# Twelve softmax scalings go from VectorE to GpSimd in a fused two-layer transformer kernel

## The chip, the cores and the metric

The kernel runs on one core of one Trainium2 chip. The metric is the device time of one execution in microseconds, as the median of three runs. Engine names are those of the profile: PE is TensorE (PEld its weight loads), DVE is VectorE, ACT is ScalarE, POOL is GpSimd, and SP is the engine that issues most DMAs.

## The reference

Two transformer layers work on 512 tokens of width 1024. The first layer mixes tokens by a spatial gating unit, the second by causal attention with a forgetting gate; both also have four heads of attention over 256 memory vectors, and both end in a gated feed-forward part. The change touches the second layer's attention alone, which has 12 heads of width 64:

```python
def forgetting_attention(q, k, v, log_f):
    c = jnp.cumsum(log_f, axis=1)
    ...
    def block(args):                       # one of four blocks of 128 query tokens
        logits = jnp.einsum('bthd,bshd->bhts', qi, k).astype(jnp.float32) * scale
        logits = logits + ci[..., :, None] - cT[..., None, :]
        logits = jnp.where(mask, logits, -jnp.inf)
        p = jax.nn.softmax(logits, axis=-1).astype(v.dtype)
        return jnp.einsum('bhts,bshd->bthd', p, v)
```

Everything is float32.

## The kernel before

**Products.** A float32 product is made of three matmuls on parts: each operand is split into a high part, cast by ACT (`whi`, L275), and a low part, the rest, subtracted by DVE (`wlo`, L276). Such a triple is what L218 to L220 show. The splits of weights, queries, keys and transposed softmax rows are most of the work of ACT and DVE.

**A forgetting head** (`FoxHead`) works on four token blocks `tb` = 0 to 3 of 128 queries each. Since attention is causal, block `tb` has rows of 128·(`tb`+1) keys, so block 3 is the longest, 128x512. The steps of a head are these.

- S3, S2, S1, S0 (`logits`): two matmuls make the block's logits `lg` in PSUM (L534, L535); one DVE instruction adds the mask, writes the rows to a tile `p` in SBUF and takes their maximum `nmx` (L543); ACT makes the exponential in place and its sum `sm` (L545). Block 0 lies in the same tile as block 2.
- N2 and N0 (`norm`; N3 and N1 do nothing): DVE takes the reciprocal of two blocks' sums at once (L477) and scales each block's rows by it (L479), the higher block first. N2 serves blocks 3 and 2, N0 serves 1 and 0.
- T0, T1, T2 (`transpose`, `turn`): PE turns the 128x128 pieces of `p` into a PSUM tile `tr` (L486), from which ACT and DVE make the parts `pT`. T0 takes the first key block of all four token blocks, so it needs all of N2 and N0; T1 and T2 take the rest.
- V0, V1, V2 (`values`): PE multiplies `pT` with the values into `o` (L559). ACT and DVE bring `o` to the tile `f` (L454, L455).

**Order.** `attend` writes the steps of head n and of head n−1's T and V steps into one list, with pieces of other matmul work (projections of queries, keys and values in the early heads, `qk` and `v`; the output projection, `y`, in the late ones) put between them. The framework's scheduler then sets each engine's order from dependencies and its own costs; each engine runs its own queue in that order and waits at semaphores.

```python
steps = ("T0", "S3", "F0", "T1", "S2", "N3", "F1", "V0", "S1", "N2", "T2", "F2", "S0", "N1", "V1", "N0",
         "F3", "V2", "F4")
```

**GpSimd** has little in this stage: for each head two small DMAs (`head_sums`, L1570 and L1571) that bring the gate's sums to the tiles `qc` and `kc` for the head after next, each held until the older head's logits have been read.

Functions that the diff touches, with the profile's line numbers (in the changed kernel, lines behind the two new ones are one or two higher: L479 becomes L480, L486 L487, L534 L536, L543 L545, L545 L547, L559 L561):

Of the kernel before, what the change touches and what calls it, by code (L numbers as in the profile page):

```python
# [43 lines left out]
def hybrid(ctx: ExitStack, tc: tile.TileContext, i: dict, out: bass.AP):  # L44
# [36 lines left out]
    V, A, PE, G = nc.vector, nc.scalar, nc.tensor, nc.gpsimd  # L81
# [209 lines left out]
    class Norm:  # L291


        def __init__(self, width=T):
            self.r4 = small("r4")
            self.acc, self.width = None, width
# [161 lines left out]

    class Softmax:


        def __init__(self):
            self.nmx, self.sm = small("nmx"), small("sm")
# [9 lines left out]
        def norm(self, tb):  # L473

            if tb % 2:
                return
            V.reciprocal(self.sm[:, tb : tb + 2], self.sm[:, tb : tb + 2])  # L477
            for x in (tb + 1, tb):
                V.tensor_scalar_mul(self.p[x], self.p[x], self.sm[:, x : x + 1])  # L479

        def turn(self, n, pieces):

# [9 lines left out]
    class MemHead(Softmax):  # L492
# [15 lines left out]
        def transpose(self, b):  # L508
            self.turn(b, [self.p[tb][:, b * P : (b + 1) * P] for tb in range(TB)])
# [10 lines left out]
    class FoxHead(Softmax):  # L520

        TURNS = ((0,), (1, 3), (2,))

        def __init__(self, pr, j, vals, dst):
            super().__init__()
# [22 lines left out]
        def transpose(self, b):  # L548
            self.turn(b, [self.p[tb][:, sb * P : (sb + 1) * P] for sb in self.TURNS[b] for tb in range(sb, TB)])

        def values(self, b):
            if b == 0:
                self.o = ps("mm", s="o")
            at = 0
            for sb in self.TURNS[b]:
                n = T - sb * P
# [1188 lines left out]
```

## Time and profile before

| | |
|---|---|
| time, median of 3 runs | 1086.39 us (1085.83 to 1086.45) |
| time of the profiled execution | 1085.8 us |
| its span, first to last instruction | 1084.1 us, at a granted clock of 0.998 |
| PE, DVE, ACT, POOL busy, share of the span | 99%, 87%, 68%, 7% |
| the 12 forgetting heads | about 598 to 706 us of the span |
| DVE busy in these 108 us | 97.94 us |
| POOL busy in these 108 us | 13.05 us |

A row of the timeline gives the start in us, the duration in us, the engine, the line, the operation, output and inputs, the shape, and how many like instructions were merged; idle time of the engine ahead of it and what ended that stand in brackets. A matmul's end is modelled, so the pace of PE is read from starts. On DVE too an instruction's duration overlaps the start of the next a little, so its cost to the queue is the distance from start to start.

### The profile page before, as it was taken

To read this page: it belongs to the slowest core of one execution; us is meant where nothing else is said; L and a number is where in the kernel's file an instruction comes from. 1 tells how busy PE (TensorE), PEld (TensorE's weight loads), DVE (VectorE), ACT (ScalarE), POOL (GpSimd) and SP (SyncE) were. 2 spreads that over 40 slices of the span, in tenths; PEclk is the share of its full clock that TensorE was granted. 3 is DMA by queue.
4 is the path that set the end of the run, shared out by engine and by line. 5 is a ranking of instruction groups with operands and counts; after the bars stand their busy time and mean duration, and the time that the engine had idled before them with its cause. 6 is when DMAs were issued, how large, how long until landed. Compare 5 with 4: busy or idle time off the path is not lost.

```text
span 1084.1 us, 19973 instructions
## 1 busy us (share of the span) xinstructions
PE 1074.6 (99%) x7224; PEld 981.8 (91%) x7224; DVE 944.6 (87%) x1893; ACT 737.1 (68%) x1605; POOL 72.7 (7%) x98
## 2 busy tenths in 40 slices
PE   9999999999999999999999999999999999999997
PEld 7998889999999988998988998889999999988996
DVE  7889659999989999986987899959999988999975
ACT  8776468766666677666765677758766666667563
POOL 0101011000000000000110111001000000000000
PEclk9999999999999999999999999999999999999999
DMA  7456666967664976364441754535867653646332
GB/s 274 160 143 167 192 166 199 247 180 209 165 179 144 272 207 215 107 202 130 128 128 47 208 128 114 151 98 185 242 196 195 165 160 115 174 130 202 107 118 78
DMA packets 131835, 179.52 MB, mean 166 GB/s; under 512 B 9948, under 2 KB 93928, under 8 KB 131736
## 3 DMA queue, kind: packets, MB, share of 16 engines
q1 hardware_dynamic: 119608, 160.66, 47.0%
q0 software_dynamic: 11712, 17.40, 10.1%
q8 instruction: 57, 0.93, 0.4%
q14 instruction: 42, 0.34, 0.1%
q10 hardware_dynamic: 416, 0.18, 0.1%
HBM read 158.71 MB, written 43.00 MB: 186 GB/s over the span
## 4 chain that ended last, share of the span: by engine, by line
PE 93%; issue 2%; DVE 2%; ACT 1%; DMA 1%; POOL 0%; SPq 0%; POOLq 0%; DVEq 0%; ACTq 0%
PE a L218 7%; PE a L219 7%; PE a L220 7%; PE y L218 4%; PE y L219 4%; PE y L220 4%; PE e L218 4%; PE e L219 3%; PE e L220 3%; PE ps L218 3%; PE ps L220 3%; PE ps L219 3%; PE p L218 3%; PE p L220 3%; PE p L219 3%; PE x L218 3%
## 5 line engine op out<-in xcount | busy, mean ns | idle before, releaser
L276 DVE TENSOR_TENSOR wlo<-raw,whi 128x512 fp32r<-128x512 f32 x316 | 211.0, 686 | 21.6 <-ACT whi L275 18.2
L275 ACT CAST whi<-raw 128x512 fp32r<-128x512 f32 x316 | 189.0, 618 | 57.8 <-PE a L219 15.0
L218 PE MATMUL a<-xshi,whi 128*128 128x256 f32 x480 | 135.2, 282 | 0.0
L219 PE MATMUL a<-xslo,whi 128*128 128x256 f32 x480 | 134.9, 281 | 0.0
L220 PE MATMUL a<-xshi,wlo 128*128 128x256 f32 x480 | 134.7, 281 | 0.0
L275 ACT CAST whi<-room 128x512 fp32r<-128x512 f32 x160 | 98.2, 621 | 48.1 <-PE x L219 9.6
L276 DVE TENSOR_TENSOR wlo<-room,whi 128x512 fp32r<-128x512 f32 x160 | 108.8, 687 | 6.4 <-ACT whi L275 3.9
L218 PEld LDWEIGHTS a<-xshi,whi 128*128 128x128 f32 x480 | 90.3, 188 | 1.8 <-ACT e L1119 1.0
L219 PEld LDWEIGHTS a<-xslo,whi 128*128 128x128 f32 x480 | 90.4, 188 | 0.7
L220 PEld LDWEIGHTS a<-xshi,wlo 128*128 128x128 f32 x480 | 90.4, 188 | 0.0
L218 PE MATMUL ps<-xshi,whi 128*128 128x256 f32 x192 | 54.3, 288 | 0.3 <-ACT whi L275 0.2
L220 PE MATMUL ps<-xshi,wlo 128*128 128x256 f32 x192 | 53.9, 284 | 0.0
L219 PE MATMUL ps<-xslo,whi 128*128 128x256 f32 x192 | 53.8, 282 | 0.0
L275 ACT CAST ff<-u 128x256 fp32r<-128x256 f32 x80 | 32.3, 406 | 29.1 <-PE p L220 15.1
L218 PE MATMUL y<-whi,mixedhi 128*128 128x512 f32 x128 | 51.2, 400 | 0.0
L219 PE MATMUL y<-wlo,mixedhi 128*128 128x512 f32 x128 | 50.7, 396 | 0.0
L218 PE MATMUL p<-whi,ff 128*128 128x512 f32 x128 | 50.5, 396 | 0.0
L220 PE MATMUL y<-whi,mixedlo 128*128 128x512 f32 x128 | 50.4, 394 | 0.0
L219 PE MATMUL p<-wlo,ff 128*128 128x512 f32 x128 | 50.3, 393 | 0.0
L220 PE MATMUL p<-whi,ff 128*128 128x512 f32 x128 | 50.2, 395 | 0.0
L219 PE MATMUL x<-xslo,whi 128*128 128x256 f32 x160 | 45.1, 282 | 0.0
L219 PE MATMUL e<-t,whi 128*128 128x256 f32 x160 | 45.1, 282 | 0.0
(376 smaller groups left out, 3573.5 us busy)
## 6 DMA issues: line engine op xcount, KB each, us to landing
room<-in_w_up SPq DMA_DIRECT2D x36, 512.0 KB, 4.1
raw<-in_w_gate SPq DMA_DIRECT2D x24, 512.0 KB, 4.3
raw<-in_w_down SPq DMA_DIRECT2D x20, 512.0 KB, 4.4
sums<-in_w_gate SPq DMA_DIRECT2D x16, 512.0 KB, 6.0
sums<-in_w_gate POOLq DMA_DIRECT2D x16, 512.0 KB, 7.0
raw<-in_w_out SPq DMA_DIRECT2D x16, 512.0 KB, 3.9
sums<-in_w_down SPq DMA_DIRECT2D x32, 256.0 KB, 5.4
sums<-in_w_down POOLq DMA_DIRECT2D x16, 512.0 KB, 7.8
```

The lines of the kernel that those rows point to most:

```text
L218: PE.matmul(o, w[0], x[0], start=start, stop=False, skip_group_check=more)
L219: PE.matmul(o, w[0], x[1], start=False, stop=False, skip_group_check=more)
L220: return PE.matmul(o, w[1], x[0], start=False, stop=stop, skip_group_check=more)
L275: last_hi[0] = A.copy(hi, src)
L276: last_split[0] = last_hi[0], (eng or V).tensor_sub(lo, src, hi)
```

## The change

The scaling of block 3 of each forgetting head, a 128x512 instruction, is issued on GpSimd; blocks 2, 1 and 0 stay on VectorE, and so do the memory heads.

```diff
     class Softmax:
 
+        by_pool = None
 
         def __init__(self):
...
             V.reciprocal(self.sm[:, tb : tb + 2], self.sm[:, tb : tb + 2])
             for x in (tb + 1, tb):
-                V.tensor_scalar_mul(self.p[x], self.p[x], self.sm[:, x : x + 1])
+                (G if x == self.by_pool else V).tensor_scalar_mul(self.p[x], self.p[x], self.sm[:, x : x + 1])
...
     class FoxHead(Softmax):
 
         TURNS = ((0,), (1, 3), (2,))
+        by_pool = 3
```

What it does to the queues is read from the order of the built programs. On GpSimd, from the DMAs for head 1 on, there stood DMAs alone:

```order
L1570 DMA qc_7663<-cc 2x512
L1571 DMA kc_7665<-cc 2x512
L1570 DMA qc_7662<-cc 2x512
L1571 DMA kc_7664<-cc 2x512
L1570 DMA qc_7663<-cc 2x512
L1571 DMA kc_7665<-cc 2x512
```

The same place now, heads 0 and 1 (`p_7820` and `p_7931` are their blocks 3, `sm_7671` and `sm_7673` the reciprocals):

```order
L1572 DMA qc_7663<-cc 2x512
L1573 DMA kc_7665<-cc 2x512
L480 TENSOR_SCALAR p_7820<-p_7820,sm_7671 128x512
L1572 DMA qc_7662<-cc 2x512
L1573 DMA kc_7664<-cc 2x512
L480 TENSOR_SCALAR p_7931<-p_7931,sm_7673 128x512
L1572 DMA qc_7663<-cc 2x512
L1573 DMA kc_7665<-cc 2x512
```

One scaling a head has come between the pairs of DMAs, twelve in all, and DVE has twelve instructions fewer. Up to head 6 the order of PE and ACT is as before and DVE differs by little more than those instructions; from head 7 on the scheduler set the engines' orders anew. On VectorE, before, from head 9's N2 (`p_8907`, `p_8930`) to its N0 (`p_8957`, `p_8930`); `p_9020` is head 10's block 3:

```order
L479 TENSOR_SCALAR p_8907<-p_8907,sm_7689 128x512
L479 TENSOR_SCALAR p_8930<-p_8930,sm_7689 128x384
L543 ISA p_8930,nmx_7688<-lg_8974,mask 128x128
L543 ISA nmx_7688 128x1
L455 TENSOR_TENSOR f_8997<-o_8951,f_8997 64x512
L276 TENSOR_TENSOR wlo_9077<-raw_9074,whi_9076 128x512
L477 RECIPROCAL sm_7689<-sm_7689 128x2
L543 ISA p_9020,nmx_7690<-lg_9017,mask 128x512
L543 ISA nmx_7690 128x1
L479 TENSOR_SCALAR p_8957<-p_8957,sm_7689 128x256
L479 TENSOR_SCALAR p_8930<-p_8930,sm_7689 128x128
```

And the same place now:

```order
L480 TENSOR_SCALAR p_8930<-p_8930,sm_7689 128x384
L545 ISA p_8930,nmx_7688<-lg_8974,mask 128x128
L545 ISA nmx_7688 128x1
L276 TENSOR_TENSOR wlo_9077<-raw_9074,whi_9076 128x512
L455 TENSOR_TENSOR f_8997<-o_8951,f_8997 64x512
L478 RECIPROCAL sm_7689<-sm_7689 128x2
L276 TENSOR_TENSOR wlo_9081<-raw_9074,whi_9080 128x512
L480 TENSOR_SCALAR p_8957<-p_8957,sm_7689 128x256
L480 TENSOR_SCALAR p_8930<-p_8930,sm_7689 128x128
L545 ISA p_9020,nmx_7690<-lg_9017,mask 128x512
```

The 512-wide scaling is gone, head 10's masking now comes behind N0 and not ahead of it, and a weight split (`wlo_9081`) has come ahead. On PE, before, ahead of head 9's T0 (`tr_9008`); `lg_9058` is head 10's S1:

```order
L220 MATMUL y_9048<-whi_8870,mixedlo_7316 128x512
L218 MATMUL y_9048<-whi_8874,mixedhi_7543 128x512
L219 MATMUL y_9048<-wlo_8875,mixedhi_7543 128x512
L220 MATMUL y_9048<-whi_8874,mixedlo_7544 128x512
L534 MATMUL lg_9058<-ka_8934,qa_8933 128x256
L535 MATMUL lg_9058<-kc_7664,qc_7662 128x256
L218 MATMUL y_9048<-whi_8880,mixedhi_8040 128x512
L486 MATMUL tr_9008<-ident,p_8930 128x128
L486 MATMUL tr_9008<-ident,p_8957 128x128
```

And now:

```order
L220 MATMUL y_9048<-whi_8870,mixedlo_7316 128x512
L487 MATMUL tr_9008<-ident,p_8930 128x128
L487 MATMUL tr_9008<-ident,p_8957 128x128
L487 MATMUL tr_9008<-ident,p_8930 128x128
L487 MATMUL tr_9008<-ident,p_8907 128x128
L487 MATMUL tr_9033<-ident,p_8957 128x128
L487 MATMUL tr_9033<-ident,p_8930 128x128
L487 MATMUL tr_9033<-ident,p_8907 128x128 x2
L218 MATMUL y_9048<-whi_8874,mixedhi_7543 128x512
```

Four 512-wide and two 256-wide matmuls that stood ahead of the turn now stand behind it. In the same way the next head's two logits matmuls have gone behind T0 in heads 7 (256 wide), 8 and 10 (512 wide), in head 7 with one 512-wide matmul of a key projection.

## The prediction

> **What bounds the kernel now.** I read the page's totals and its chain first, then the busy time by stretches of the forgetting heads, then who waited there. The page, parts 1 and 4:
>
> ```profile
> PE 1074.6 (99%) x7224; PEld 981.8 (91%) x7224; DVE 944.6 (87%) x1893; ACT 737.1 (68%) x1605; POOL 72.7 (7%) x98
> PE 93%; issue 2%; DVE 2%; ACT 1%; DMA 1%; POOL 0%; SPq 0%; POOLq 0%; DVEq 0%; ACTq 0%
> ```
>
> PE sets the time: 93% of the chain that ended last. A modelled busy share proves little by itself, so I look at the stage. Busy time by stretch (start and end; length; then PE, PEld, DVE, ACT, POOL):
>
> ```profile
> 611.00:635.00 24.00, 24.00 (x145) 21.23 (x144) 23.42 (x68) 18.21 (x46) 3.47 (x6) 1.00 0.64 169
> 662.50:695.00 32.50, 32.41 (x178) 27.05 (x177) 32.01 (x91) 27.85 (x70) 3.17 (x6) 1.00 0.58 154
> sum 108.00, PE 107.91 PEld 95.91 DVE 97.94 ACT 79.70 POOL 13.05; mean PE 21.58 PEld 19.18 DVE 19.59 ACT 15.94 POOL 2.61
> ```
>
> In heads 1 to 3 (611 to 635 us) and 7 to 10 (662.5 to 695) DVE is full as well, with 0.58 and 0.49 us free. So DVE could be the engine that holds PE. The waits of PE's weight loads between 598 and 706 us, which stand for PE's own, tell whether it does (total, times, longest):
>
> ```profile
> PEld tr L486 <- PE lg L535: 0.5, 1, 0.5
> PEld o L559 <- DVE pT L276: 0.4, 2, 0.3
> PEld o L559 <- ACT pT L275: 0.4, 1, 0.4
> ```
>
> They come to 1.3 us in four waits. DVE is full but just keeps up. That is the most a freer DVE can give back here, 0.12% of the time: the upper bound of any gain.
>
> **What goes from DVE.** The twelve scalings as one group (busy, mean ns of one), and one of them with the instruction behind it:
>
> ```profile
> L479 DVE TENSOR_SCALAR p<-p,sm 128x512 f32<-128x512 f32 x12 | 5.8, 481 | 0.1
> 687.85 0.48 DVE L479 TENSOR_SCALAR p<-p,sm 128x512 f32<-128x512 f32 x1
> 688.25 0.68 DVE L276 TENSOR_TENSOR pT<-tr,pT 128x512 fp32r<-128x512 f32 x1
> ```
>
> From start to start one costs the queue 0.40 us, so 12 x 0.40 = 4.8 us leave DVE. Beside PE's work this is worth nothing by itself; it counts only where PE waits for DVE.
>
> **What comes to GpSimd.** The trace has no scaling on GpSimd. The nearest rows are its passes over SBUF tiles, and rows where it met DVE:
>
> ```profile
> 2.08 0.61 POOL L105 TENSOR_SCALAR_AFFINE_SELECT tri<-ones 128x512 fp32r<-128x512 f32 x1
> 38.26 1.10 POOL L726 TENSOR_SCALAR_AFFINE_SELECT wsf<-wsf 128x768 f32<-128x768 f32 x1 [2.09 <-DMA wsf<-in_w_sp]
> ...
> 37.22 0.69 DVE L395 TENSOR_TENSOR q<-q,q 64x512 fp32r<-64x512 f32 x1
> ...
> 38.66 1.24 DVE L395 TENSOR_TENSOR q<-q,q 64x512 fp32r<-64x512 f32 x1
> ...
> 718.51 0.69 DVE L276 TENSOR_TENSOR wlo<-raw,whi 128x512 fp32r<-128x512 f32 x1
> 718.68 0.96 POOL L289 TENSOR_TENSOR r<-v,mhalf 128x1 f32<-128x1 f32 x1 [37.17 <-DVE v L889]
> ```
>
> One scaling takes GpSimd between 0.61 us (a like pass over the same size) and 1.10 us (a pass over a tile half as wide again, with a wait in it). I take 0.61, the nearest in size. The Trainium skill ("GPSIMD Engine Reference", section 4.1) says that one-input work runs there at roughly line rate; with its 1.2 GHz I estimate 0.43 us for 512 elements, and then DVE would stand less and the sum below would end nearer its lower end. No row here goes that low.
>
> The rows also show that the two engines block each other. DVE's subtraction at 38.66, with two inputs in SBUF, took 1.24 us and not 0.69 while GpSimd went over its tile, and ended 0.54 us after it: it stood until GpSimd was done. The other way round, GpSimd's small power at 718.68 took 0.96 us behind a split that ended at 719.20. So the 0.40 us saved is set against DVE standing behind GpSimd. Per head this lies between 0 (GpSimd runs beside a mask or a `pT`, whose first input is in PSUM) and 1.10 (a split or a scaling behind all of it). By the order, a 384-wide scaling or a split stands next to it in nearly every head. I take 0.20 to 0.40: a third to two thirds of 0.61. DVE's net gain per head is then 0 to 0.2 us, and PE is left as it is.
>
> **Is block 3 ready in time?** The rows around the end of heads 7 and 8, the reciprocal of N2, the scalings of N0 and PE's T0:
>
> ```profile
> 667.33 0.16 DVE L477 RECIPROCAL sm<-sm 128x2 f32<-128x2 f32 x1
> ...
> 669.38 0.53 DVE L479 TENSOR_SCALAR p<-p,sm 128x256 f32<-128x256 f32 x2
> ...
> 670.36 1.03 PE L486 MATMUL tr<-ident,p 128*128 128x128 f32 x8
> ...
> 675.42 0.54 DVE L479 TENSOR_SCALAR p<-p,sm 128x256 f32<-128x256 f32 x2
> ...
> 676.27 1.04 PE L486 MATMUL tr<-ident,p 128*128 128x128 f32 x8
> ```
>
> The two logits matmuls and the one `qk` matmul that now stand behind head 7's T0 are worth 2 x 0.12 + 0.23 = 0.47 us (paces in the rows of the next fence), so PE asks for block 3 at 669.89, 2.4 us after the reciprocal's end at 667.49. GpSimd needs at most a split's 0.69 us of waiting and 1.10 of work, 1.8. It is in time, and its two DMAs for later heads, queued behind the scaling, are late by no more than that, for logits a whole head later.
>
> **The turn moved ahead.** T0 also needs N0, whose chain is mask, exponential, reciprocal, scaling. Heads 9 and 10, with PE's pace in the logits matmuls:
>
> ```profile
> 684.52 0.40 ACT L545 ACTIVATE p<-p,nmx 128x128 f32<-128x128 f32 x1
> 685.05 0.17 DVE L477 RECIPROCAL sm<-sm 128x2 f32<-128x2 f32 x1
> 685.15 0.69 DVE L543 CUSTOM_DVE_ANT_0 p<-lg,mask 128x512 f32<-128x512 f32 x1
> 685.77 0.55 DVE L479 TENSOR_SCALAR p<-p,sm 128x256 f32<-128x256 f32 x2
> ...
> 686.05 0.28 PE L534 MATMUL lg<-ka,qa 128*128 128x256 f32 x1
> 686.17 0.29 PE L535 MATMUL lg<-kc,qc 68*128 68x256 f32 x1
> ...
> 686.53 1.04 PE L486 MATMUL tr<-ident,p 128*128 128x128 f32 x8
> ...
> 693.14 0.40 PE L534 MATMUL lg<-ka,qa 128*128 128x512 f32 x1
> 693.17 0.55 DVE L479 TENSOR_SCALAR p<-p,sm 128x256 f32<-128x256 f32 x2
> 693.38 0.40 PE L535 MATMUL lg<-kc,qc 68*128 68x512 f32 x1
> 693.87 0.96 PE L486 MATMUL tr<-ident,p 128*128 128x128 f32 x7
> ```
>
> - Head 9: four matmuls of 0.23 and two of 0.12 us, 1.16 us, go behind T0, so PE asks at 686.53 − 1.16 = 685.37. N0 ended at 685.77 + 0.55 = 686.32. It gets earlier by up to 0.48, since ACT's exponential now stands ahead of a copy of `y` (0.48 us to the queue), and the mask that leaves N0's front is replaced by a split of about the same length. That leaves 686.32 − 0.48 − 685.37 = 0.47 us of wait with DVE relieved, 0.95 without either.
> - Heads 7 and 8: PE asks at 669.89 and, with two matmuls of 0.23 less, at 675.81; N0 ends at 669.91 and 675.96 less the relief. Wait 0 with a relief of 0.2, else 0.02 + 0.15 = 0.17 together.
> - Head 10: PE waited from 693.61 to 693.87, 0.26 us. Its logits pair moves too, so PE asks at 693.15, but in the new orders two splits and two casts have left N0's chain, over 1 us. The wait goes.
>
> **The sum.** On the path: −0.26 (head 10), +0.47 to +0.95 (head 9, I take 0.65), 0 to +0.17 (heads 7 and 8, I take 0.1). That is +0.5 us. Bounds from these terms: −1.3 if every wait in the stage goes, +2.0 if GpSimd takes somewhat more of DVE than I assume. The profiled execution took 1085.8 us (its span of 1084.1 and 1.7 around it), 0.6 below the median of the runs shown, so +0.5 is 1086.3 there and 1086.9 against the median of 1086.39. Changes within 0.2%, 2.2 us, are about what a measurement of this kernel can tell from no change.
>
> **Rivals.**
>
> 1. *Slower: GpSimd's passes take DVE's place in the full heads.* If one scaling takes 1.10 us and DVE stands behind all of it, each head costs DVE 1.10 − 0.40 = 0.70 us. In the seven full heads that is 4.9 us, less the 0.58 + 0.49 free: 3.8 us that PE must wait, with the 0.5 above +4.3, 1090.7 us. It decides from 0.78 us of standing per head: 7 x 0.38 − 1.07 + 0.5 is about 2.1. For it: the 1.24 us at 38.66, DVE full for 55 of the 108 us, splits all around. Against it: 0.61 us for a like pass, and DVE has many instructions with an input in PSUM. The Trainium skill's rule speaks for it ("SBUF — State Buffer", Who interferes with whom): a DVE instruction in a two-port mode, or with two SBUF inputs against a GpSimd one that reads SBUF, fully blocks while the other holds the shared ports. The row at 38.66 agrees; that a one-input scaling on DVE is blocked in this way is not shown by the rows above. Chance 0.34.
> 2. *Block 3 comes late.* Above 1.6 us per scaling with 0.7 of waiting, T0 of heads 3, 7 and 8 waits for GpSimd as well, and rival 1's loss is in full force: over 4.3 us slower, above 1091. No pass in the trace is that long. Chance 0.04.
> 3. *Faster.* The 4.8 us come back because PE's modelled ends hide waits. At PE's steady pace of 0.23 us per 512 columns I see none beyond the 1.3 us; −2.2 us would need almost twice that, 1084.2 or less. Chance 0.04.
> 4. That the change does not do what it says is out: the built order shows twelve scalings on GpSimd.
>
> **Chances and range.** The forecast, within 2.2 us of before, has what is left: 0.58. The range goes down to 1086.39 − 1.3 = 1085.1. Upward it reaches into rival 1, as far as 1090.2, which leaves out its upper end and rival 2, some 0.16. The forecast's own range is 1085.1 to 1088.4. Faster by over 0.2%: 0.04; within: 0.58; slower: 0.38.
>
> **What would show it.** Right: twelve GpSimd rows of about 0.6 us for `p<-p,sm`; DVE busy in the heads down by 2 to 5 us; waits of PE's weight loads still near 1 to 2 us; head 10's gap ahead of T0 gone and one of about 0.6 ahead of head 9's. Wrong by rival 1: GpSimd rows over 1 us, DVE's 384-wide scalings and splits beside them stretched by more than 0.4, and PE waiting in every full head for `pT` or N0. Wrong by rival 2: T0 waiting for GpSimd itself. Wrong the other way: these waits gone and the stage shorter by over 2 us.

## The result, and the profile after

The changed kernel takes 1087.39 us (median of 20 runs, 1086.98 to 1088.68), the kernel before 1085.91 us beside it (1085.03 to 1087.04). The ratio is 1.0016, with a 95% interval of 1.0010 to 1.0022: 1.5 us slower, clear of noise, but within the 0.2% that the prediction called no change. The profiled execution took 1087.28 us, its span 1085.3.

Part 1 of the page after, then the twelve passes as one group of GpSimd's instructions (busy, mean ns of one), then the busy time by stretches as in the prediction (length; PE, PEld, DVE, ACT, POOL):

```profile
PE 1075.0 (99%) x7224; PEld 981.4 (90%) x7224; DVE 943.5 (87%) x1881; ACT 736.5 (68%) x1605; POOL 94.0 (9%) x110
...
L480 POOL TENSOR_SCALAR p<-p,sm 128x512 f32<-128x512 f32 x12 | 21.1, 1755 | 45.3 <-DVE sm L478 35.7 <-DVE nmx L545 9.5
...
611.00:635.00 24.00, 23.04 (x137) 20.00 (x136) 23.34 (x64) 17.30 (x46) 8.30 (x9) 1.00 0.61 163
...
662.50:695.00 32.50, 32.07 (x176) 26.62 (x175) 30.79 (x86) 26.86 (x68) 10.53 (x10) 1.00 0.58 150
...
sum 108.00, PE 106.62 PEld 94.47 DVE 96.34 ACT 78.87 POOL 34.00; mean PE 21.32 PEld 18.89 DVE 19.27 ACT 15.77 POOL 6.80
```

One scaling takes GpSimd 1.755 us, nearly three times the 0.61 of the prediction. DVE, rid of twelve instructions, is busy for only 1.6 us less (96.34 against 97.94), and PE for 1.3 us less: it waits more. The waits between 590 and 710 us, PEld's rows first, then PE's (total, times, longest):

```profile
PEld tr L487 <- PE qk L220: 1.4, 1, 1.4
PEld o L561 <- DVE pT L276: 0.9, 3, 0.4
PEld tr L487 <- issue: 0.6, 1, 0.6
PEld o L561 <- ACT pT L275: 0.3, 1, 0.3
...
PE tr L487 <- DVE p L480: 1.2, 2, 1.0
```

One wait of 1.0 us stands out: a T0 waits for a scaling that DVE itself makes. It is head 2's; rows of GpSimd, DVE and PE there:

```profile
622.96 0.54 POOL L1572 DMA_DIRECT2D qc<-cc  x1 [5.55 <-PE o L561]
623.54 1.57 POOL L480 TENSOR_SCALAR p<-p,sm 128x512 f32<-128x512 f32 x1
...
623.33 2.00 DVE L480 TENSOR_SCALAR p<-p,sm 128x384 f32<-128x384 f32 x1
625.25 0.27 DVE L545 CUSTOM_DVE_ANT_0 p<-lg,mask 128x128 f32<-128x128 f32 x1
...
626.58 0.55 DVE L480 TENSOR_SCALAR p<-p,sm 128x256 f32<-128x256 f32 x2
...
627.28 0.63 PE L487 MATMUL tr<-ident,p 128*128 128x128 f32 x4 [0.96 <-DVE p L480]
```

In head 2 alone the pass stands between the two DMAs of one pair, not between two pairs as in the order shown for heads 0 and 1. So GpSimd had a small DMA to issue, until 623.50, and then its pass from 623.54 to 625.11. DVE's scaling of block 2, an instruction of 0.42 us, started at 623.33 and ended at 625.33, 0.22 us behind that pass. Everything behind it (block 0's mask, its exponential, N0) came late, and T0 with it.

To say where PE falls back I number its matmuls and compare their starts with those of the kernel before. Up to the stage the two profiled executions differ by 0.39 us; that arises in the first 50 us, where both have the same instructions, and says nothing. From there PE loses 1.15 us in heads 0 to 6, 1.12 of it at head 2's T0, 0.36 in heads 7 to 11, and 0.16 behind the stage. Little comes to it behind that; over the last 60 matmuls single executions scatter by up to 0.4 us, also those of kernels without GpSimd's passes.

### The profile page after: what moved, and what is told of

The parts are those of the page before. It is cut to its first block, busy times and chain, and to the rows that moved or that the text cites. A ratio compares the mean times of both kernels' runs of the same rounds, so it can differ in the third digit from the quotient of the medians.

```text
span 1085.3 us, 19991 instructions
## 1 busy us (share of the span) xinstructions
PE 1075.0 (99%) x7224; PEld 981.4 (90%) x7224; DVE 943.5 (87%) x1881; ACT 736.5 (68%) x1605; POOL 94.0 (9%) x110
## 4 chain that ended last, share of the span: by engine, by line
PE 93%; issue 2%; DVE 2%; ACT 1%; DMA 0%; POOL 0%; SPq 0%; POOLq 0%; DVEq 0%; ACTq 0%
PE a L218 7%; PE a L219 7%; PE a L220 7%; PE y L218 4%; PE y L219 4%; PE y L220 4%; PE ps L218 4%; PE ps L220 4%; PE e L218 4%; PE e L219 3%; PE e L220 3%; PE ps L219 3%; PE p L218 3%; PE p L220 3%; PE p L219 3%; PE x L218 3%
```

## The experiments

Times are medians; each kernel's *before* was timed beside it on the same chip. The three columns on the right are what PE loses in the profiled execution in heads 0 to 6 (PE's matmuls 4000 to 4440 of 7224), in heads 7 to 11 (to 4720) and behind them (to 5000).

| kernel | us | before | ratio (95%) | heads 0-6 | heads 7-11 | behind |
|---|---|---|---|---|---|---|
| the change | 1087.39 | 1085.91 | 1.0016 (1.0010 to 1.0022) | +1.15 | +0.36 | +0.16 |
| early | 1086.90 | 1086.01 | 1.0010 (1.0001 to 1.0019) | +1.15 | +0.01 | +0.14 |
| late | 1086.50 | 1086.01 | 1.0005 (0.9996 to 1.0014) | -0.01 | +0.36 | +0.14 |
| no2 | 1086.36 | 1086.01 | 1.0004 (0.9996 to 1.0013) | +0.01 | +0.38 | +0.14 |
| drop | 1085.40 | 1086.01 | 0.9995 (0.9986 to 1.0004) | +0.01 | -0.25 | -0.02 |
| n3 | 1086.74 | 1086.12 | 1.0005 (0.9996 to 1.0014) | +0.10 | +0.26 | +0.15 |
| act | 1085.78 | 1086.12 | 0.9997 (0.9988 to 1.0006) | +0.38 | -0.11 | -0.02 |
| n3act | 1086.52 | 1086.12 | 1.0004 (0.9996 to 1.0013) | +0.27 | +0.74 | 0.00 |
| sums4 | 1086.35 | 1086.14 | 1.0002 (0.9992 to 1.0011) | +0.01 | +0.52 | +0.13 |

A single ratio here rarely tells two neighbours apart, since its interval is about 1 us to each side; the starts of PE's matmuls do. The times follow the three columns' sum, to about 0.6 us.

**Which heads: early, late, no2.** A line in `FoxHead` chooses the heads (the condition below is early's; late has `>= 7`, no2 has `!= 2`).

```
             self.pr, self.j, self.vals, self.dst = pr, j, vals, dst
             self.blocks = (0, 1, 2)
+            self.by_pool = 3 if 2 * pr + j < 7 else None
```

> GpSimd scales block 3 in heads 0 to 6 only; PE's and ACT's order is then that of the kernel before. Place theory (GpSimd's pass of about 1.6 us holds up a DVE scaling that T0 waits for; in the trace of the change PE fell back by 1.1 us at head 2's T0 and by 0.4 net behind head 6): +1.1 us against before, 1.0 to 1.3. Order theory (the loss comes from T0 written earlier from head 7 on): 0, within 0.3. Even theory (each of the twelve passes costs DVE about the same, PE pays later): +0.8 to +1.0.

> GpSimd scales block 3 in heads 7 to 11 only; PE's and ACT's order is that of the changed kernel. Place theory: +0.4 us against before, 0.2 to 0.7. Order theory: +1.5. Even theory: +0.6 to +0.7, and the same wait in front of T0 in each of the heads.

> GpSimd scales block 3 in all heads but head 2; PE's and ACT's order is that of the changed kernel. Place theory: +0.4 us against before, 0.2 to 0.8, the 1.1 of head 2 gone; if the loss only moves to a neighbouring head, +1.0 or more. Order theory: +1.5. Even theory: +1.4.

The place theory holds, to a few hundredths in PE's starts: in the twelve heads early loses 1.15 us at head 2 and nothing else, late has the 0.36 of heads 7 to 11, and no2 gets the 1.15 back without a neighbour paying for it. In the times it holds within 0.2 us, but they alone would not decide: early's +0.9 lies just below the place theory's range and in the even theory's. The order theory falls with early, which has PE's and ACT's order of the kernel before and still loses the 1.15; the even theory falls with no2, where eleven of the twelve passes cost a quarter of the time lost.

**Without the scaling: drop.**

```
-                (G if x == self.by_pool else V).tensor_scalar_mul(self.p[x], self.p[x], self.sm[:, x : x + 1])
+                if x != self.by_pool:
+                    V.tensor_scalar_mul(self.p[x], self.p[x], self.sm[:, x : x + 1])
```

> Block 3 is not scaled at all in the twelve heads (that part of the computation is left out); the orders of PE, ACT and DVE are those of the changed kernel. What is left is the relief of DVE and the new order. Place theory: between -0.8 and +0.3 us against before, all of the loss being GpSimd's passes. Order theory: +1.2 to +1.5. The prediction's own sum, which had the order at +0.5 with a small relief: 0 to +0.5, with a wait of up to 0.6 us ahead of head 9's T0.

The sum row between 598 and 706 us, and PEld's waits there:

```profile
sum 108.00, PE 107.92 PEld 95.96 DVE 93.93 ACT 79.04 POOL 12.71; mean PE 107.92 PEld 95.96 DVE 93.93 ACT 79.04 POOL 12.71
...
PEld o L562 <- DVE pT L276: 0.7, 3, 0.3
PEld o L562 <- ACT pT L275: 0.3, 1, 0.3
PEld tr L488 <- issue: 0.2, 1, 0.2
```

With the new order and the relief alone DVE is busy for 4.0 us less, and PE gains 0.24 us in the stage, not more: the relief was never worth much, as the prediction had it. The difference to the change, 1.75 us in the stage (1.14 and 0.61), is what GpSimd's passes cost. No wait of T0 for a scaling is left.

**What a pass is and whom it holds: bench.** Behind the kernel's end, one case after the other, each started by a small DVE product:

```
+        for w in (128, 256, 384, 512):
+            G.tensor_scalar_mul(g[:, :w], g[:, :w], s[-1])
+            close_trial(g)
...
+        G.tensor_scalar_mul(g, g, s[-1])
+        for n in range(6):
+            V.tensor_scalar_mul(v[n][:, :384], v[n][:, :384], s[-1])
+        close_trial(g, v[5])
```

> The changed kernel with a series of measured cases behind its end, on tiles of their own (its time as a whole says nothing): GpSimd scaling 128 to 512 columns alone, 512 columns by a constant, DVE scaling 384 columns six times alone, and then beside a GpSimd pass: six such DVE scalings, four DVE products of two SBUF inputs, four with the first input in PSUM, three ACT scalings, and one DVE scaling that starts at three different points of the pass. Port theory (GpSimd's scaling of 512 columns is about 1.56 us by itself, and only DVE instructions that read and write SBUF alone are held): 1.5 to 1.6 us alone, DVE scalings beside it stretched by 0.4 to 1.6 in all, nothing lost with the input in PSUM or on ACT. Slow-by-meeting theory (a pass is 0.6 us alone and long only because DVE holds it up): 0.6 to 0.7 alone.

GpSimd alone (L1714; L1716 by a constant); six DVE scalings alone (L1719), and the same six (L1723) with GpSimd's pass beside them (L1721); four DVE instructions with an input in PSUM (L1731) and the pass beside them (L1729); the pass beside ACT (L1733); and a DVE scaling (L1740) that comes 0.47 us into the pass (L1738):

```profile
1084.80 0.61 POOL L1714 TENSOR_SCALAR bg<-bg,bs 128x128 f32<-128x128 f32 x1 [5.37 <-DVE bs L1703]
1085.70 0.92 POOL L1714 TENSOR_SCALAR bg<-bg,bs 128x256 f32<-128x256 f32 x1 [0.29 <-DVE bs L1709]
1086.91 1.24 POOL L1714 TENSOR_SCALAR bg<-bg,bs 128x384 f32<-128x384 f32 x1 [0.29 <-DVE bs L1709]
1088.44 1.56 POOL L1714 TENSOR_SCALAR bg<-bg,bs 128x512 f32<-128x512 f32 x1 [0.29 <-DVE bs L1709]
1090.28 1.49 POOL L1716 TENSOR_SCALAR bg<-bg 128x512 f32<-128x512 f32 x1 [0.28 <-DVE bs L1709]
...
1092.00 2.07 DVE L1719 TENSOR_SCALAR bv<-bv,bs 128x384 f32<-128x384 f32 x6
1094.30 2.84 DVE L1723 TENSOR_SCALAR bv<-bv,bs 128x384 f32<-128x384 f32 x6
1094.43 1.84 POOL L1721 TENSOR_SCALAR bg<-bg,bs 128x512 f32<-128x512 f32 x1 [2.66 <-DVE bs L1709]
...
1100.90 2.73 DVE L1731 SCALAR_TENSOR_TENSOR bv<-bp,bs,bv 128x512 f32<-128x512 f32 x4
1101.04 1.56 POOL L1729 TENSOR_SCALAR bg<-bg,bs 128x512 f32<-128x512 f32 x1 [1.42 <-DVE bs L1709]
...
1104.06 1.56 POOL L1733 TENSOR_SCALAR bg<-bg,bs 128x512 f32<-128x512 f32 x1 [1.46 <-DVE bs L1709]
...
1108.86 1.56 POOL L1738 TENSOR_SCALAR bg<-bg,bs 128x512 f32<-128x512 f32 x1 [0.55 <-DVE bs L1709]
1109.33 0.43 DVE L1740 TENSOR_SCALAR bq<-bq,bs 128x384 f32<-128x384 f32 x1 [0.64 <-ACT bq L1739]
```

The pass is slow by itself: 1.56 us with nothing beside it. Beside DVE scalings, which have one input and that in SBUF, DVE loses 0.77 us and GpSimd 0.28. Beside instructions with an input in PSUM, and beside ACT, GpSimd loses nothing, and the four DVE instructions (2.73 us) start an even 0.66 us apart. Beside four DVE products of two SBUF inputs (3.17 us; they were not timed alone) the pass took 2.05. So the port theory holds for which instructions meet. How long DVE is held is another matter: the six scalings lose half a pass, not a whole one as in head 2, and of the three single scalings, one that came with the pass, one 0.47 us into it (0.43 us) and one behind it, none was held.

**The moment: sums4.** In head 2 GpSimd's small DMA is issued right ahead of the pass. Here SP issues it (with its twin):

```
-            G.dma_start(qc[66:68, :].bitcast(F32), cc[n : n + 33 : 32, :].bitcast(F32))
-            G.dma_start(kc[64:66, :].bitcast(F32), cc[64 + n : 64 + n + 33 : 32, :].bitcast(F32))
+            E = nc.sync if n == 4 else G
+            E.dma_start(qc[66:68, :].bitcast(F32), cc[n : n + 33 : 32, :].bitcast(F32))
+            E.dma_start(kc[64:66, :].bitcast(F32), cc[64 + n : 64 + n + 33 : 32, :].bitcast(F32))
```

> The changed kernel, with only the two small DMAs for head 4's sums (the ones in GpSimd's queue on both sides of head 2's scaling) issued by SP; the orders of PE, DVE and ACT are those of the changed kernel. GpSimd then starts head 2's pass some 0.4 us earlier, beside a DVE instruction that reads PSUM, and not 0.13 us behind the start of DVE's scaling. Moment theory (the 1.15 us of head 2 hang on the moment at which the pass meets DVE's scaling): that scaling takes about 0.85 us as in heads 0, 1 and 4, not 2.0, and the time falls by 0.8 to 1.2 us against the change: +0.2 to +0.7 against before. Place theory (head 2 has no room for any pass): +1.2 to +1.6 against before.

Head 2's pass and DVE's scaling there:

```profile
623.45 1.56 POOL L480 TENSOR_SCALAR p<-p,sm 128x512 f32<-128x512 f32 x1 [5.62 <-DVE sm L478]
...
623.74 0.60 DVE L480 TENSOR_SCALAR p<-p,sm 128x384 f32<-128x384 f32 x1
```

This execution runs 0.41 us behind that of the change from its first 50 us on, so the pass starts 0.50 us earlier than in the change and DVE's scaling in the same place. The pass is as long as before, and DVE's scaling beside it takes 0.60 us instead of 2.00 (0.85 was expected). Head 2's 1.15 us are gone, the kernel is at +0.2 us against before, although heads 7 to 11 cost 0.16 more in its profiled execution than in the change's. So head 2 has room for a pass; what cost was the moment, or the DMA ahead.

**Which of the two: sweep and sweep2.** Both put cases behind the kernel's end; sweep2 adds the first line.

```
+            G.dma_start(v[1][66:68, len(s) : len(s) + 1], row[64:66, len(s) - 1 : len(s)])
             G.tensor_scalar_mul(g, g, s[-1])
...
             for n in range(k):
                 V.tensor_copy(row[:, 18 + n : 19 + n], s[-1])
             V.tensor_scalar_mul(v[0][:, :384], v[0][:, :384], s[-1])
             V.tensor_scalar_mul(q[:, :384], q[:, :384], s[-1])
```

> The changed kernel with sixteen cases behind its end (its time as a whole says nothing): a GpSimd scaling of 128x512 and two DVE scalings of 128x384 on other tiles, the DVE ones put off by 0 to 7 small copies, eight times by themselves and eight times behind a DVE product with an input in PSUM. Moment theory: DVE's delay depends on where in the pass its scaling comes: 0 where DVE is first, about 0.4 in most places, and the whole pass (1.4 to 1.6 us) in a narrow stretch. If a pass always holds the port in pieces of about 0.4 us, no delay is over 0.5 us, and head 2's 2.0 us stay unexplained.

> The changed kernel with fourteen cases behind its end (its time as a whole says nothing): as in the sweep before, but GpSimd has a small DMA (2x1) to issue right ahead of its 128x512 scaling, as it has in head 2, and the DVE scalings of 128x384 are put off by 0 to 13 small copies, about 0.06 us each. Hand-over theory (the DMA issue holds the port too, and a DVE scaling that comes in its last part stands behind the issue and the whole pass): one to three neighbouring cases show a DVE scaling of 1.6 to 2.1 us, the others at most 0.9. If the DMA ahead has no part in it: no DVE scaling over 0.9 us, and head 2's hold stays open.

In sweep no DVE scaling was held for longer than 0.44 us at any of the sixteen moments: the moment theory, in this form, fails. Its first case, one of the longest holds:

```profile
1085.79 1.69 POOL L1715 TENSOR_SCALAR bg<-bg,bs 128x512 f32<-128x512 f32 x1 [5.39 <-DVE bs L1703]
...
1085.96 0.85 DVE L1721 TENSOR_SCALAR bq<-bq,bs 128x384 f32<-128x384 f32 x1
```

DVE's scaling ended at 1086.81, the pass at 1087.48: DVE got through in the middle of the pass. So it went in eleven of the twelve cases with a held scaling, which ended 0.89 to 1.11 us after the pass's start; the twelfth came 1.02 us into the pass and stood to its end. In sweep2 the picture of head 2 is back. Two of its cases, GpSimd's issue and pass and then DVE's scalings:

```profile
1105.35 0.69 POOL L1715 DMA_DIRECT2D bv<-bs  x1 [0.68 <-DVE bs L1709]
1106.07 1.58 POOL L1716 TENSOR_SCALAR bg<-bg,bs 128x512 f32<-128x512 f32 x1
...
1105.86 1.14 DVE L1722 TENSOR_SCALAR bq<-bq,bs 128x384 f32<-128x384 f32 x1
...
1111.44 0.54 POOL L1715 DMA_DIRECT2D bv<-bs  x1 [0.77 <-DVE bs L1709]
1112.01 1.58 POOL L1716 TENSOR_SCALAR bg<-bg,bs 128x512 f32<-128x512 f32 x1
...
1111.74 2.06 DVE L1721 TENSOR_SCALAR bv<-bv,bs 128x384 f32<-128x384 f32 x1
```

In six of the fourteen cases (put off by 8 to 13 copies) the first DVE scaling started between 0.30 us ahead of the issue's end and right behind it, and took 1.47 to 2.06 us; in two (6 and 7 copies; the first of the two shown has 7) the second took 1.13 and 1.14; in the remaining six none took over 0.43. The expectation named at most three neighbouring cases and 0.9 us for the rest, so the stretch is wider than I thought. In four of the eight (9, 10, 12 and 13 copies) DVE's scaling ended 0.21 to 0.23 us behind the pass, as in head 2; in the other four it ended 0.46 to 0.65 us ahead of the pass's end.

So the hand-over theory holds in part. The DMA ahead of the pass has a part in the hold, and a DVE scaling that comes while GpSimd issues it can stand through the issue and the whole pass. It need not. The change itself has two more places of the kind, heads 3 and 8, where the pass stands directly behind a pair of DMAs; head 3's second DMA, DVE's scaling of block 2 and the pass:

```profile
632.49 0.54 POOL L1573 DMA_DIRECT2D kc<-cc  x1
...
632.79 0.42 DVE L480 TENSOR_SCALAR p<-p,sm 128x384 f32<-128x384 f32 x1
...
633.07 1.61 POOL L480 TENSOR_SCALAR p<-p,sm 128x512 f32<-128x512 f32 x1
```

DVE's scaling started 0.24 us ahead of the issue's end (in head 8 0.03) and was not held, nor were the second scalings in sweep2's cases of 3 to 5 copies, which started 0.19 to 0.27 us ahead of it. What decides between these outcomes, and how a pass without an issue lets DVE through in its middle, is open.

**Earlier, or on ACT: n3, act, n3act.** In n3 the pass stands in N3, behind a reciprocal of its own; act gives the twelve scalings to ACT in N2; n3act gives them to ACT in N3. The core of n3, and act's line:

```
+            if tb == self.by_pool:
+                V.reciprocal(self.sm[:, tb : tb + 1], self.sm[:, tb : tb + 1])
+                G.tensor_scalar_mul(self.p[tb], self.p[tb], self.sm[:, tb : tb + 1])
```

```
+                    A.activation(self.p[x], self.p[x], AF.Copy, scale=self.sm[:, x : x + 1])
```

> GpSimd scales block 3 as in the change, but in N3, right behind a reciprocal of its own (one DVE instruction of 0.16 us more per head), so that it no longer starts beside DVE's scaling of block 2. Place theory (what counts is that DVE's next scaling of N2 meets the pass): between -0.6 and +0.6 us against before. Load theory (each pass costs DVE the same wherever it lies): +1.3 to +2.0.

> ACT makes the twelve scalings of block 3 (about 0.7 us each) in place of GpSimd, in N2. Port theory: no DVE instruction is held, so the stage keeps drop's gain where ACT has room: between -0.6 and +0.3 us against before. ACT theory: the next exponential of the head stands behind the scaling, N0 and T0 come later by 0.5 us or more in the full heads: +0.6 to +3.

> ACT makes the twelve scalings of block 3, in N3, behind a reciprocal of their own. Port theory: between -0.6 and +0.3 us against before, at least as fast as with the scaling in N2. ACT theory: the exponential of block 2 or 1 stands behind the scaling: +0.6 to +3.

The twelve scalings in n3 (GpSimd) and in act (ACT), and two of PE's waits in n3act:

```profile
L478 POOL TENSOR_SCALAR p<-p,sm 128x512 f32<-128x512 f32 x12 | 18.7, 1560 | 52.2 <-DVE sm L477 52.1
```

```profile
L481 ACT ACTIVATE p<-p,sm 128x512 f32<-128x512 f32 x12 | 8.6, 716 | 0.0
```

```profile
PEld lg L541 <- issue: 0.8, 1, 0.8
...
PE lg L541 <- DMA ka<-whi: 0.3, 1, 0.3
```

n3 is at +0.36 us in the stage, and its passes never wait (1560 ns each); in time it is at +0.6, the edge of the place theory's range. The load theory's 1.3 lies just inside the interval of the time, but far from the starts. n3 is not a clean trial, though: DVE's scaling of block 2 still meets the pass in heads 3, 5, 6 and 9 and takes 0.66 to 0.88 us there instead of 0.42. act is at +0.27 in the stage and -0.3 in time, within the port theory's range, but it loses 0.38 at head 3's T0, in the way of the ACT theory. The scaling, block 0's exponential behind it, and DVE's reciprocal of N0, which waits for that:

```profile
632.75 0.71 ACT L481 ACTIVATE p<-p,sm 128x512 f32<-128x512 f32 x1
...
633.37 0.39 ACT L550 ACTIVATE p<-p,nmx 128x128 f32<-128x128 f32 x1
...
633.88 0.17 DVE L478 RECIPROCAL sm<-sm 128x2 f32<-128x2 f32 x1 [0.85 <-ACT p L550]
```

So ACT has no room there, and the gain of drop does not show. n3act is inconclusive: +0.4 in time, between the two theories, and +1.0 in the stage, where PE also waited 0.3 us for a key transfer; that wait was not followed further. None of the kernels that compute everything is faster than the kernel before by more than its interval.

## Why the prediction was right, and where its steps were not

The time lies in the range and within 0.2%, as forecast, at +1.5 us instead of +0.5. Of the prediction's own signs of being right only the end of head 10's gap came: the passes take 1.755 us and not about 0.6, DVE is busy for 1.6 us less and not 2 to 5, PE's weight loads wait for 3.4 us and not 1 to 2, and head 9 has no gap. Step by step:

- **Right: a freer DVE is worth at most 1.3 us.** drop shows 0.24.
- **Wrong: one scaling takes GpSimd 0.61 us, 1.10 at most.** It is 1.56 alone and 1.755 in the kernel. The step took the price of another operation of the same size, and its bound from a larger one of the same other operation. The Trainium skill ("GPSIMD Engine Reference", section 4.1), whose rate the prediction had set beside this, calls one-input work roughly line-rate; bench disagrees: 1.56 us, against 0.48 for the same scaling on DVE in the kernel before.
- **Right on average, wrong in spread: DVE stands 0.2 to 0.4 us per head.** Each DVE instruction that met a pass, against the median of its like: 0.43, 0.43, 1.58, 0.41 in heads 0, 1, 2 and 4; 0.41, 0.10, 0.21, 0.06 in heads 7 to 10; nothing in the other four. That is 3.6 us, 0.30 per head. The average is right by luck: the pass is nearly three times as long as assumed, and DVE stands for 0.17 of it instead of a third to two thirds. And one head takes 1.58 of it, and only what a T0 waits for costs time. An average per head, set against the relief of 0.40 per head, said that PE is left as it is; head 2 alone cost it 1.15.
- **Right, but not by its bound: block 3 is in time.** No wait names GpSimd. It was close: the pass is longer than the 1.6 us of rival 2, and in head 7, where the prediction gave GpSimd at most 1.8 us from the reciprocal's end, it took 2.26 (from 668.25); it ends at 670.51, 0.11 us before PE is through with the matmul ahead of T0 (670.39 and its pace of 0.23). The rows of GpSimd, DVE, PE's last `qk` matmul and T0 there:

```profile
668.43 2.08 POOL L480 TENSOR_SCALAR p<-p,sm 128x512 f32<-128x512 f32 x1 [1.02 <-DVE sm L478]
...
669.89 0.95 DVE L480 TENSOR_SCALAR p<-p,sm 128x256 f32<-128x256 f32 x2
...
670.39 0.40 PE L220 MATMUL qk<-shi,wlo 128*128 128x512 f32 x1
...
670.99 1.06 PE L487 MATMUL tr<-ident,p 128*128 128x128 f32 x8 [0.21 <-DVE p L480]
```

- **The turn moved ahead.** Head 10's gap of 0.26 us ahead of T0 went, as forecast. Head 7's T0 waits 0.37, where the prediction had 0 to 0.17 for heads 7 and 8 together, since N0's first scaling took 0.77 us instead of 0.35 beside the pass; in drop there is no gap there. Head 9's wait of 0.47 to 0.95 did not come, in the change or in drop: N0 came earlier by more than the 0.48 that the prediction gave it (in drop it ends 0.24 us ahead of T0).
- **The sum.** Order and relief: forecast +0.5, measured by drop -0.24. GpSimd's passes on the path: forecast 0, measured 1.75. The errors have opposite signs, so that the number came near is luck.
- **Rival 1** named the right engine and mechanism, an engine standing for the other's port, but charged it to all seven full heads alike: 0.70 us in each. The measured standing was 2.8 us in those seven, 0.40 per head, below the 0.78 from which it was to decide. Two of its signs came, passes over 1 us and DVE scalings stretched by more than 0.4 (in five heads); the third, PE waiting in every full head, did not. The Trainium skill's rule ("SBUF — State Buffer", Who interferes with whom) says that against a DVE instruction in a two-port mode the second comer blocks until the first has finished, and that GpSimd's descriptor generation for a DMA needs time on the port too. Head 2 and four cases of sweep2 agree with both; sweep and the other four held cases of sweep2 do not agree with the first, since there DVE got through 0.46 to 0.80 us before the pass ended.

The 0.13 to 0.16 us behind the stage appear in every kernel with GpSimd scalings and in none without. There the small power on GpSimd at 739 us takes 0.80 us instead of 0.54, beside a DVE instruction with two inputs, in each of the kernels with the loss. ACT's `y` (L910), which needs the power, starts 0.03 us behind it, and ACT's weight cast behind that is what PE waits for, 0.24 us, at 741.71. Why the two meet differently there was not settled.

## What to carry to other kernels

An instruction moved to GpSimd needs the price of that operation on that engine; a like-sized pass of another kind can be off by a factor of two and a half. What the move cost here was not its mean contention but the one meeting that a waiting chain runs through, so look for the place where GpSimd issues a DMA or starts its pass just as DVE reaches an SBUF-only instruction on the path: there DVE can be held for a whole pass, though not each such meeting held it. And moving a DMA off GpSimd's queue there can be worth more than moving the work.

## What the runs showed of the hardware that I had not expected

- A GpSimd scaling of 128 rows took 0.61, 0.92, 1.24 and 1.56 us for 128 to 512 float32 columns: 2.5 ns a column and 0.29 us ahead of it, and 1.49 us for 512 by a constant. The mask-making pass over 128x512 in the same kernel took 0.61 us.
- A DVE scaling of 0.41 us was held for up to 0.44 us by a pass alone (sweep), and for up to 1.65 us by a pass directly behind a DMA issue (sweep2). Without an issue ahead DVE mostly got through 0.9 to 1.1 us after the start of the pass, ahead of its end (eleven of the twelve held scalings of sweep).
